# Low parts of the weights by an adding transfer instead of a subtraction on VectorE, and another order in the first stage

## The chip, the cores and the metric

The kernel runs on one core of a Trainium2 chip. The metric is the device time of one execution in microseconds; before the change the median of three runs is 983.17 us (983.04 to 983.79). A core has TensorE (PE, matmuls; PEld is its loading of stationary operands), VectorE (DVE), ScalarE (ACT), GpSimd (POOL) and SyncE (SP). Each works off its own instructions in order; they meet at semaphores. Transfers are issued by SP or by GpSimd and run on 16 DMA engines.

## The reference

One encoder layer on 512 tokens of width 1024, in float32: a layer norm, one input projection whose columns feed a gated convolution and attention with three groups of dilated windows, an output projection, a layer norm, a gated feed-forward block with a convolution, and a last layer norm.

```python
h = layer_norm(x, ln0_g, ln0_b)
proj = h @ w_in + b_in
y_a = (gate_b * dwconv3(gate_c * hin, conv_w)) @ w_a
# attention: three groups, combined with softmax weights over their denominators
y_b = comb.reshape(bsz, seq, ATT_GROUP_W) @ w_b
mix = (g_a * y_a + g_b * y_b) @ w_o + b_o
h = layer_norm(ALPHA * h + mix, ln1_g, ln1_b)
up = h @ w_up + b_up
f = gelu(dwconv3(a, ffn_conv_w) + ffn_conv_b) * gte
h = layer_norm(ALPHA * h + f @ w_down + b_down, ln2_g, ln2_b)
```

## The kernel before

Every matmul operand is a float32 value held as two fp32r values, a high part (hi) and a low part (lo, the value minus hi). A product is three matmuls, high x high, high x low, low x high (`mm3`, L357 to L360); a unit is 8 such triples over the depth of 1024, 24 matmuls of 512 columns.

The weights lie in memory as 82 chunks (0 to 81) of 2048 columns (some of 1536) in the order of use. A chunk is two halves of 1024 columns. `load` (L265) has SP fetch the halves into `raw`, three buffers. `split` (L279) has ScalarE copy a half into `hi` (L292; three buffers of 2048 columns), and `low` (L297) has VectorE write `lo = raw - hi` (L298; five buffers of 1024 columns). `chunk` (L304) is called where a chunk is first used: it splits this one and the next and loads the one after. A buffer that is taken again waits until TensorE has finished with its old content: the low half that comes five halves later. Only the last chunk's low halves lie in buffers of their own (`blk`).

Stages: first layer norm and the first four units, which take the tokens in two halves of 256 (`first_norm`, `first_features`, `first_products`; chunks 0 and 1); the rest of the input projection with attention jobs between its units (`slot`, L696); the convolution branch; the branch projections and gates; the output projection (chunks 44 to 47, blocks of 128 tokens); the feed-forward block in two parts of 11 pairs of units (chunks 48 on), each followed by its part of the down projection. In the output projection's second half and in the last stage (chunks 79 to 81) a block of 128 tokens goes through several chunks before the next block does.

A scheduler orders the instructions of each engine, except those marked with `pin`, which keep the order of the program; in the first stage most are pinned. In the first stage `feature_major` (L348) turns transposed x into features: ScalarE writes `lnT`, VectorE casts it to the high part (for half of the features of the first tokens ScalarE does, L352), and VectorE subtracts (L355). An attention job has its scores computed (`a`), is scaled (`b`), transposed (`b2`, copied by ScalarE to `PT`) and summed (`c`), in different steps of `slot`.

Of the kernel before, what the change touches and what calls it, by code (L numbers as in the profile page):

```python
# [7 lines left out]
AF = mybir.ActivationFunctionType  # L8
ALU = mybir.AluOpType
AX = mybir.AxisListType  # L10

P = 128
D = 1024
T = 512
KT = D // P
# [14 lines left out]
C_G0 = C_BIN + 76  # L30
# [57 lines left out]
def lay_out_weights(w):  # L88

    w_in, w_a, w_b, w_o = w["w_in"][0], w["w_a"][0], w["w_b"][0], w["w_o"][0]  # L90
    w_up, w_down = w["w_up"][0], w["w_down"][0]

    def block(m, f0, nf):
        k = m.shape[0] // P
        return m[:, f0 : f0 + nf].reshape(k, P, nf).transpose(1, 0, 2).reshape(P, k * nf)

    units = in_units()
    parts = []
    for name, key, cols in chunk_plan():
        if name == "in":  # L100
            c = [block(w_in, units[key + i][3] * P, P) for i in range(2)]
        elif name == "vt":
            g, kh = key
            c = [block(w_in[kh * 512 : (kh + 1) * 512], (BLK_V + g * 4) * P, 512)]
        elif name == "wa":
            c = [block(w_a, (key + i) * P, P) for i in range(2)]
        elif name == "wb":
            c = [block(w_b, (key + i) * P, P) for i in range(4)]
        elif name == "gate":
            c = [block(w_in, (BLK_GA + key) * P, P), block(w_in, (BLK_GB + key) * P, P)]  # L110
        elif name == "wo":
            half, kh = key
            c = [block(w_o[kh * 512 : (kh + 1) * 512], half * 512, 512)]
        elif name == "up":
            c = [block(w_up, key * P, P), block(w_up, DFF + key * P, P)]
        else:
            part, half, c0, n = key
            k0 = (part * FFH + c0) * P
            c = [block(w_down[k0 : k0 + n * P], half * 512, 512)]
        c = np.concatenate(c, axis=1)  # L120
        assert c.shape == (P, cols), (name, key, c.shape)
        parts.append(np.ascontiguousarray(c).reshape(-1))
    return np.concatenate(parts)
# [49 lines left out]
def build(tc, x, wst, colt, dist, rows, vrow, out):  # L173
# [3 lines left out]
    with ExitStack() as ctx:  # L177
# [22 lines left out]
        def ps(tag):  # L200
            return psum.tile([P, 512], F32, tag=tag, name="ps_" + tag, bufs=2)
# [55 lines left out]
        def col(c):  # L257
            return cols[:, c : c + 1]
# [19 lines left out]
        def split(i):  # L278
            if i >= len(plan) or i in splits:  # L279
                return  # L280
            load(i)
            n = plan[i][2]
            hi = whl.tile([P, 2048], F32R, tag="hi", name=f"hi{i}")
            if i == len(plan) - 1:
                los = [blk(F32R, (1024,), f"lo{i}") for _ in range(0, n, 1024)]
            else:
                los = [whl.tile([P, 1024], F32R, tag="lo", name=f"lo{i}", bufs=5) for _ in range(0, n, 1024)]
            step = 512 if i == 0 else 1024
            starts = (0, 1024, 512, 1536) if i == 0 else range(0, n, step)
            for c in starts:  # L290
                part = slice(c, min(c + step, n))
                nc.scalar.activation(hi[:, part], Pieces(raws[i])[:, part], AF.Copy)  # L292
                if i > 1:
                    low(i, hi, Pieces(los), part)
            splits[i] = (hi, Pieces(los))

        def low(i, hi, lo, part):  # L297
            ins = nc.vector.tensor_tensor(lo[:, part], Pieces(raws[i])[:, part], f(hi[:, part]), op=ALU.subtract)  # L298
            if i < 2:
                pin(ins)  # L300
# [3 lines left out]
        def chunk(name, key):  # L304
            i = where[(name, key)]
            split(i)
            split(i + 1)
            load(i + 2)
            return splits[i]
# [4 lines left out]
        def pin(ins):  # L314

            return tc.keep_in_program_order(ins) if pinned[0] else ins
# [28 lines left out]
        def normalise(z, mean, rstd):  # L345
            pin(nc.vector.tensor_scalar(z, z, mean, rstd, op0=ALU.subtract, op1=ALU.mult))

        def feature_major(pst, dst, kt, cg, cb, c0, c1, cast=False):  # L348
            t = f32t("lnT")[:, : c1 - c0]
            nc.scalar.activation(t, pst, AF.Identity, bias=col(cb + kt), scale=col(cg + kt))  # L350
            if cast:
                nc.scalar.activation(dst[:, 0, c0:c1], pst, AF.Identity, bias=col(cb + kt), scale=col(cg + kt))  # L352
            else:
                pin(nc.vector.tensor_copy(dst[:, 0, c0:c1], t))
            return pin(nc.vector.tensor_tensor(dst[:, 1, c0:c1], t, f(dst[:, 0, c0:c1]), op=ALU.subtract)).ins  # L355

        def mm3(o, ah, al, bh, bl, start, stop):  # L357
# [27 lines left out]
        def first_features(hf):  # L385
            rr = (2 * hf, 2 * hf + 1)
            for k0 in range(0, KT, 2):
                if hf == 0 and k0 % 4 == 0:

                    for n in range(2):  # L390
                        low(0, *splits[0], slice(n * 1024 + k0 * P, n * 1024 + (k0 + 4) * P))
                pst = ps(("pt", "s")[k0 // 2 % 2])
                for k in (k0, k0 + 1):
                    for r in rr:
                        o = pst[:, (k % 2) * 256 + (r % 2) * P :][:, :P]
                        nc.tensor.transpose(o, xt[r][:, k * P : (k + 1) * P], ident)
                for k in (k0, k0 + 1):
                    c = (k % 2) * 256
                    last = feature_major(pst[:, c : c + 256], hT[k], k, C_G0, C_B0, hf * 256, hf * 256 + 256, hf == 0 and k >= 4)
            return last  # L400

        def first_products(hf, n0, steps):
            w = splits[n0 // 2]
            t = slice(hf * 256, hf * 256 + 256)
            for n, k, m in steps:
                a = slice(n % 2 * 1024 + k * P, n % 2 * 1024 + (k + 1) * P)
                wk, hk = w[m // 2][:, a], hT[k][:, m % 2, t]
                nc.tensor.matmul(first[n][:, t], wk, hk, start=k == 0 and m == 0, stop=k == KT - 1 and m == 2)  # L408


        halves = []
# [5 lines left out]
        whole = [[(n, k, m) for k in range(KT) for m in range(3)] for n in range(4)]  # L417
        first_norm(0)
        with tc.issue_after(roots[0]):
            chunk("in", 0)  # L420
        first_features(0)
        first = [ps("acc"), ps("acc"), ps("u"), ps("u")]
        first_products(0, 0, halves)
        first_norm(1)
# [268 lines left out]

        wait, ready = [0], {}

        def slot(new=True):  # L696

            while vtodo:
                transpose_v(*vtodo.pop(0))
            if running:  # L700
                running.pop(0).c()
            if scaled:
                jb = scaled.pop(0)
                jb.b2()
                running.append(jb)
            if sums and ready[sums[0].key[0]] <= wait[0]:
                jb = sums.pop(0)
                jb.b()
                scaled.append(jb)
            if scores and new:  # L710
                for _ in range(2):
                    jb = scores.pop(0)
                    jb.a()
                p = jb.key[0]
                if not any(x.key[0] == p for x in scores) and jb.key[1] == 2:
                    merge(p)
                    ready[p] = wait[0] + 3
                    order = [(0, 0), (0, 1), (0, 2), (0, 3), (1, 0), (2, 0), (1, 1), (2, 1)]
                    sums.extend(alljobs[(p,) + o] for o in order)
            wait[0] += 1  # L720
            if new:
                scores.extend(late)
                late.clear()

        alljobs = {}
        for n, (kind, a0, a1, blkno) in enumerate(in_units()):
            w = chunk("in", n - n % 2)
            if n < 4:
                o = first[n]
            else:  # L730
                o = ps("acc")
                unit(o, w, (n % 2) * 1024, hT)
            slot()
            if kind == "v" and a0 > 0:
                slot(False)
            if kind in "qkv":
                evac_qkv(kind, a0, a1, blkno, o)
                if kind == "k":
                    for i in range(4 if a1 == 0 else 2):
                        alljobs[a0, a1, i] = Job(a0, a1, i)  # L740
                        late.append(alljobs[a0, a1, i])
                elif kind == "v":
                    vtodo.append((a0, a1))
            else:
                evac_conv(kind, a0, blkno, o)
            if n - 1 in V_AFTER:
                g = V_AFTER[n - 1]
                ws = [chunk("vt", (g, kh)) for kh in range(2)]
                for j in range(4):
                    o = values(g, j, ws)  # L750
                    slot()
                    evac_values(g, j, o)
# [203 lines left out]
```

## Time and profile before

| | |
|---|---|
| median of three runs | 983.17 us |
| profiled execution | 983.07 us |
| its span, first to last instruction | 981.3 us |
| TensorE busy | 964.7 us (98%) |
| VectorE busy | 551.1 us (56%) |
| ScalarE busy | 395.9 us (40%) |
| GpSimd busy | 55.3 us (6%) |
| bytes moved by transfers | 97.29 MB |
| mean granted TensorE clock | 0.998 |

The profile is of one execution. Busy time leaves out register, branch and semaphore instructions and those that issue transfers. Matmuls overlap each other: a 512-column matmul is listed with 0.39 us though one starts every 0.23 us. In a line of the trace, `lo<-raw,hi` is what is written and from what; an entry in square brackets is idle time of the engine before the instruction and what ended it.

### The profile page before, as it was taken

To read this page: it belongs to the slowest core of one execution; us is meant where nothing else is said; L and a number is where in the kernel's file an instruction comes from. 1 tells how busy PE (TensorE), PEld (TensorE's weight loads), DVE (VectorE), ACT (ScalarE), POOL (GpSimd) and SP (SyncE) were. 2 spreads that over 40 slices of the span, in tenths; PEclk is the share of its full clock that TensorE was granted. 3 is DMA by queue.
4 is the path that set the end of the run, shared out by engine and by line. 5 is a ranking of instruction groups with operands and counts; after the bars stand their busy time and mean duration, and the time that the engine had idled before them with its cause. 6 is when DMAs were issued, how large, how long until landed. Compare 5 with 4: busy or idle time off the path is not lost.

```text
span 981.3 us, 11983 instructions
## 1 busy us (share of the span) xinstructions
PE 964.7 (98%) x4713; PEld 813.5 (83%) x4713; DVE 551.1 (56%) x882; ACT 395.9 (40%) x675; POOL 55.3 (6%) x163
## 2 busy tenths in 40 slices
PE   8999999999999999999999999999999999999996
PEld 7888888788888888888888888988888888888885
DVE  6855855868675454421344667659452245454266
ACT  5553555565653333223433333544441134443220
POOL 1000000000010101001000000011000001000000
PEclk9999999999999999999999999999999999999999
DMA  7313322121222222326333321342323232322312
GB/s 276 103 50 129 96 77 66 65 88 65 65 65 86 87 86 86 107 86 214 108 106 109 108 84 46 129 171 84 110 75 97 86 129 93 101 86 96 129 38 81
DMA packets 28217, 97.29 MB, mean 99 GB/s; under 512 B 3456, under 2 KB 3968, under 8 KB 28160
## 3 DMA queue, kind: packets, MB, share of 16 engines
q1 hardware_dynamic: 25776, 89.60, 27.6%
q0 software_dynamic: 2384, 6.92, 2.2%
q8 instruction: 37, 0.61, 0.2%
q14 instruction: 20, 0.16, 0.1%
HBM read 94.36 MB, written 2.15 MB: 98 GB/s over the span
## 4 chain that ended last, share of the span: by engine, by line
PE 92%; DVE 3%; ACT 2%; DMA 2%; issue 1%; SPq 0%; DVEq 0%; ACTq 0%; POOLq 0%
PE ps_acc L358 15%; PE ps_acc L360 15%; PE ps_acc L359 15%; PE ps_u L358 5%; PE ps_s L360 5%; PE ps_s L358 5%; PE ps_s L359 5%; PE ps_u L360 5%; PE ps_u L359 5%; PE ps_pt L360 4%; PE ps_pt L358 4%; PE ps_pt L359 4%; PE ps_pt L580 1%; DMA raw<-wst 1%; PE ps_acc L408 1%
## 5 line engine op out<-in xcount | busy, mean ns | idle before, releaser
L298 DVE TENSOR_TENSOR lo<-raw,hi 128x1024 fp32r<-128x1024 f32 (+1 forms) x166 | 198.3, 1199 | 236.4 <-ACT hi L292 102.0
L292 ACT ACTIVATE hi<-raw 128x1024 fp32r<-128x1024 f32 (+1 forms) x166 | 166.9, 1034 | 248.4 <-PE ps_acc L359 73.5
L358 PE MATMUL ps_acc<-hT,hi 128*128 128x512 f32 x416 | 164.3, 395 | 0.6 <-DVE kbd L470 0.6
L360 PE MATMUL ps_acc<-hT,lo 128*128 128x512 f32 x416 | 162.3, 390 | 0.0
L359 PE MATMUL ps_acc<-hT,hi 128*128 128x512 f32 x416 | 162.0, 390 | 0.0
L360 PEld LDWEIGHTS ps_acc<-hT,lo 128*128 128x128 f32 x416 | 78.1, 188 | 16.7
L358 PEld LDWEIGHTS ps_acc<-hT,hi 128*128 128x128 f32 x416 | 78.2, 188 | 16.5 <-PE ps_pt L580 0.8
L359 PEld LDWEIGHTS ps_acc<-hT,hi 128*128 128x128 f32 x416 | 78.2, 188 | 15.5
L561 ACT ACTIVATE S<-S,nm 128x128 f32<-128x128 f32 (+2 forms) x96 | 40.1, 419 | 39.8 <-DVE nm L559 36.3
L359 PE MATMUL ps_acc<-h1T,hi 128*128 128x512 f32 (+1 forms) x96 | 36.0, 375 | 0.0
L358 PE MATMUL ps_acc<-h1T,hi 128*128 128x512 f32 (+1 forms) x96 | 35.8, 373 | 0.0
L358 PE MATMUL ps_pt<-h1T,hi 128*128 128x512 f32 (+1 forms) x96 | 35.6, 371 | 0.0
L359 PE MATMUL ps_pt<-h1T,hi 128*128 128x512 f32 (+1 forms) x96 | 35.6, 371 | 0.0
L360 PE MATMUL ps_pt<-h1T,lo 128*128 128x512 f32 (+1 forms) x96 | 35.6, 371 | 0.0
L358 PE MATMUL ps_u<-h1T,hi 128*128 128x512 f32 (+1 forms) x96 | 35.6, 371 | 0.0
L359 PE MATMUL ps_u<-h1T,hi 128*128 128x512 f32 (+1 forms) x96 | 35.6, 371 | 0.0
L360 PE MATMUL ps_u<-h1T,lo 128*128 128x512 f32 (+1 forms) x96 | 35.6, 371 | 0.0
L359 PE MATMUL ps_s<-h1T,hi 128*128 128x512 f32 (+1 forms) x96 | 35.6, 371 | 0.0
L358 PE MATMUL ps_s<-h1T,hi 128*128 128x512 f32 (+1 forms) x96 | 35.6, 371 | 0.0
L360 PE MATMUL ps_acc<-h1T,lo 128*128 128x512 f32 (+1 forms) x96 | 35.6, 371 | 0.0
L360 PE MATMUL ps_s<-h1T,lo 128*128 128x512 f32 (+1 forms) x96 | 35.6, 371 | 0.0
L659 POOL COPY fp<-fp 128x127 f32<-128x127 f32 x22 | 14.0, 635 | 318.0 <-ACT fp L885 318.0
(397 smaller groups left out, 2037.1 us busy)
## 6 DMA issues: line engine op xcount, KB each, us to landing
raw<-wst SPq DMA_DIRECT2D x160, 512.0 KB, 3.6
x<-x SPq DMA_DIRECT2D x4, 512.0 KB, 7.1
hb<-x POOLq DMA_DIRECT2D x4, 512.0 KB, 6.1
out<-hb SPq DMA_DIRECT2D x7, 256.0 KB, 2.1
ln_g<-rows POOLq DMA_DIRECT2D x3, 512.0 KB, 6.1
ln_b<-rows POOLq DMA_DIRECT2D x3, 512.0 KB, 6.9
raw<-wst SPq DMA_DIRECT2D x4, 256.0 KB, 2.6
vbias<-vrow POOLq DMA_DIRECT2D x1, 512.0 KB, 8.1
```

What stands on the lines that cost most here:

```text
L292: nc.scalar.activation(hi[:, part], Pieces(raws[i])[:, part], AF.Copy)
L298: ins = nc.vector.tensor_tensor(lo[:, part], Pieces(raws[i])[:, part], f(hi[:, part]), op=ALU.subtract)
L358: nc.tensor.matmul(o, ah, bh, start=start, stop=False)
L359: nc.tensor.matmul(o, ah, bl, start=False, stop=False)
L360: nc.tensor.matmul(o, al, bh, start=False, stop=stop)
L408: nc.tensor.matmul(first[n][:, t], wk, hk, start=k == 0 and m == 0, stop=k == KT - 1 and m == 2)
L561: nc.scalar.activation(v, v, AF.Exp, bias=nm[:, j : j + 1], scale=0.125, accum_out=dn[:, j : j + 1])
L580: nc.tensor.transpose(pt[:, j * P : (j + 1) * P], self.pe[:, j * P : (j + 1) * P], ident)
L659: nc.gpsimd.tensor_copy(u[:, 1:128], u[:, 512:639])
```

## The change

`split` no longer calls `low` for chunks 2 to 81. After each copy to `hi`, ScalarE writes the negated value into `lo`, rounded as `hi` is, so it is minus the high part, and GpSimd issues a transfer of the same weights from memory that adds to what stands in `lo`. Chunks 0 and 1 still go through VectorE. Chunk 0 is laid out by quarters, so that its first half holds the first four depth tiles of both units; its second half is copied to `hi` after the first four features; its low parts are made a quarter at a time; VectorE makes all casts of the features. The first products are pinned by their first matmul, chunk 1 is split after the first features, and chunk 2 is loaded there. `slot` finishes all running jobs and takes one scaling step, or two after the units of v, where there was an extra step without scores.

```diff
+            if key == 0:
+                c = [b[:, h : h + 512] for h in (0, 512) for b in c]
...
-            step = 512 if i == 0 else 1024
-            starts = (0, 1024, 512, 1536) if i == 0 else range(0, n, step)
-            for c in starts:
-                part = slice(c, min(c + step, n))
+            if i == 0:
+                splits[i] = (hi, Pieces(los))
+                return
+            for c in range(0, n, 1024):
+                part = slice(c, min(c + 1024, n))
                 nc.scalar.activation(hi[:, part], Pieces(raws[i])[:, part], AF.Copy)
                 if i > 1:
-                    low(i, hi, Pieces(los), part)
+                    l = Pieces(los)[:, part]
+                    nc.scalar.activation(l, Pieces(raws[i])[:, part], AF.Copy, scale=-1.0)
+                    src = wst[int(offs[i]) : int(offs[i + 1])].rearrange("(p c) -> p c", p=P)
+                    nc.gpsimd.dma_start(out=l, in_=src[:, part], accum_op=ALU.add)
             splits[i] = (hi, Pieces(los))
+
+        def first_high(half):
+
+            for n in range(2):
+                part = slice(half * 1024 + n * 512, half * 1024 + (n + 1) * 512)
+                pin(nc.scalar.activation(splits[0][0][:, part], Pieces(raws[0])[:, part], AF.Copy))
...
-            nc.scalar.activation(t, pst, AF.Identity, bias=col(cb + kt), scale=col(cg + kt))
-            if cast:
-                nc.scalar.activation(dst[:, 0, c0:c1], pst, AF.Identity, bias=col(cb + kt), scale=col(cg + kt))
-            else:
-                pin(nc.vector.tensor_copy(dst[:, 0, c0:c1], t))
+            pin(nc.scalar.activation(t, pst, AF.Identity, bias=col(cb + kt), scale=col(cg + kt)))
+            pin(nc.vector.tensor_copy(dst[:, 0, c0:c1], t))
...
-                if hf == 0 and k0 % 4 == 0:
-
-                    for n in range(2):
-                        low(0, *splits[0], slice(n * 1024 + k0 * P, n * 1024 + (k0 + 4) * P))
+                if hf == 0:
+
+                    if k0 == 4:
+                        first_high(1)
+                    c = k0 // 4 * 1024 + k0 // 2 % 2 * 512
+                    low(0, *splits[0], slice(c, c + 512))
...
-            chunk("in", 0)
+            split(0)
+            first_high(0)
         first_features(0)
+        split(1)
+        load(2)
...
-            if running:
+            while running:
                 running.pop(0).c()
-            if scaled:
+            while scaled:
                 jb = scaled.pop(0)
                 jb.b2()
                 running.append(jb)
-            if sums and ready[sums[0].key[0]] <= wait[0]:
-                jb = sums.pop(0)
-                jb.b()
-                scaled.append(jb)
+            for _ in range(more):
+                if sums and ready[sums[0].key[0]] <= wait[0]:
+                    jb = sums.pop(0)
+                    jb.b()
+                    scaled.append(jb)
...
-            slot()
-            if kind == "v" and a0 > 0:
-                slot(False)
+            slot(2 if kind == "v" and a0 > 0 else 1)
```

How the instructions stand on ScalarE at the start, before: `hi0` is the high part of chunk 0, `lnT` the features that come out of the transposes in `ps_pt` and `ps_s`.

```order
L330 ACTIVATE l00mv_179<-l00mv_179,eps_98 128x2
L292 ACTIVATE hi0_191<-raw0_86 128x512 x2
L292 ACTIVATE hi0_191<-raw0_89 128x512 x2
L350 ACTIVATE lnT_214<-ps_pt_209,cols_78 128x256
L350 ACTIVATE lnT_218<-ps_pt_209,cols_78 128x256
L350 ACTIVATE lnT_227<-ps_s_222,cols_78 128x256
L350 ACTIVATE lnT_231<-ps_s_222,cols_78 128x256
```

The same place on ScalarE now:

```order
L342 ACTIVATE l00mv_179<-l00mv_179,eps_98 128x2
L307 ACTIVATE hi0_191<-raw0_86 128x512 x2
L362 ACTIVATE lnT_202<-ps_pt_197,cols_78 128x256
L362 ACTIVATE lnT_206<-ps_pt_197,cols_78 128x256
L362 ACTIVATE lnT_216<-ps_s_211,cols_78 128x256
L362 ACTIVATE lnT_220<-ps_s_211,cols_78 128x256
L307 ACTIVATE hi0_191<-raw0_89 128x512 x2
```

The two copies of the second half of `raw0` have moved behind the first four features.

On ScalarE behind the first units, before: `kbd0` holds the keys, `vT00` the first values, which TensorE transposes next, `hi3` the high part of chunk 3.

```order
L468 ACTIVATE kbd0_104<-ps_acc_264,cols_78 64x4x128 x2
L292 ACTIVATE hi3_591<-raw3_442 128x1024
L474 ACTIVATE vT00_551<-ps_u_265,cols_78 128x4x112
L475 ACTIVATE vT00_551<-ps_u_265,cols_78 128x4x16
L292 ACTIVATE hi3_591<-raw3_444 128x1024
```

And now:

```order
L485 ACTIVATE kbd0_104<-ps_acc_264,cols_78 64x4x128 x2
L295 ACTIVATE hi3_593<-raw3_444 128x1024
L298 ACTIVATE lo3_594<-raw3_444 128x1024
L491 ACTIVATE vT00_553<-ps_u_265,cols_78 128x4x112
L492 ACTIVATE vT00_553<-ps_u_265,cols_78 128x4x16
L295 ACTIVATE hi3_593<-raw3_446 128x1024
```

The negated part of chunk 3 (L298) stands between the keys and the values.

On ScalarE at the end, before: the high parts of the last chunks, 79 to 81.

```order
L292 ACTIVATE hi79_7340<-raw79_7288 128x1024
L292 ACTIVATE hi79_7340<-raw79_7290 128x1024
L292 ACTIVATE hi80_7395<-raw80_7347 128x1024
L292 ACTIVATE hi80_7395<-raw80_7349 128x1024
L292 ACTIVATE hi81_7406<-raw81_7402 128x1024
L292 ACTIVATE hi81_7406<-raw81_7404 128x512
```

And now, with the negated parts:

```order
L298 ACTIVATE lo79_7496<-raw79_7444 128x1024
L298 ACTIVATE lo80_7552<-raw80_7503 128x1024
L295 ACTIVATE hi80_7551<-raw80_7503 128x1024
L295 ACTIVATE hi80_7551<-raw80_7505 128x1024
L298 ACTIVATE lo81_7565<-raw81_7560 128x1024
L298 ACTIVATE lo81_7566<-raw81_7562 128x512
L298 ACTIVATE lo80_7553<-raw80_7505 128x1024
L295 ACTIVATE hi81_7564<-raw81_7560 128x1024
```

The second low half of chunk 80 stands behind both of chunk 81, and GpSimd's transfers to them stand in the same order.

## Rows read from the trace of the kernel before

**Rows 1.** Page, part 1: span, and each engine's busy us (share) xinstructions
```profile
span 981.3 us, 11983 instructions
...
PE 964.7 (98%) x4713; PEld 813.5 (83%) x4713; DVE 551.1 (56%) x882; ACT 395.9 (40%) x675; POOL 55.3 (6%) x163
```

**Rows 2.** Waits of PE: who waited for whom: us in total, times, longest us
```profile
PE ps_pt L396 <- DVE x L346: 2.2, 2, 1.1
PE ps_u L358 <- ACT PT L582: 2.1, 2, 1.6
PE ps_u L408 <- ACT hi L292: 1.1, 1, 1.1
```

**Rows 3.** Windows: the stretch, then each engine's busy us in it
```profile
core 0: us, PE busy (x) PEld busy (x) DVE busy (x) ACT busy (x) POOL busy (x), PEclk, DMA share, GB/s
10.00:30.00 20.00, 16.75 (x128) 15.17 (x128) 15.07 (x34) 11.71 (x21) 0.40 (x2) 1.00 0.52 205
...
120.00:250.00 130.00, 127.13 (x664) 107.86 (x663) 91.42 (x184) 76.09 (x181) 6.14 (x14) 1.00 0.23 72
...
635.00:930.00 295.00, 295.00 (x1304) 244.36 (x1303) 143.69 (x159) 110.19 (x140) 23.17 (x83) 1.00 0.33 107
```

**Rows 4.** Lines: groups, busy us, mean ns; third row from 120 to 250 us
```profile
L298 DVE TENSOR_TENSOR lo<-raw,hi 128x1024 fp32r<-128x1024 f32 (+1 forms) x166 | 198.3, 1199 | 236.4 <-ACT hi L292 102.0 <-PE ps_acc L360 50.6 <-PE ps_s L359 28.6
L292 ACT ACTIVATE hi<-raw 128x1024 fp32r<-128x1024 f32 (+1 forms) x166 | 166.9, 1034 | 248.4 <-PE ps_acc L359 73.5 <-PE ps_s L360 48.3 <-PE ps_u L360 39.7
L292 ACT ACTIVATE hi<-raw 128x1024 fp32r<-128x1024 f32 x18 | 18.6, 1058 | 13.7 <-PE ps_acc L359 9.8 <-issue 2.9 <-ACT S L561 0.9
```

**Rows 5.** Timeline of PE, ACT and DVE, first stage: start, duration, what
```profile
10.77 0.55 PE L396 MATMUL ps_pt<-cols,x 128*128 128x128 f32 x3
...
11.23 1.15 ACT L292 ACTIVATE hi<-raw 128x512 fp32r<-128x512 f32 x2 [2.04 <-DMA raw<-wst]
12.29 1.00 ACT L350 ACTIVATE lnT<-ps_pt,cols 128x256 f32<-128x256 f32 x2
...
10.63 0.68 DVE L298 TENSOR_TENSOR lo<-raw,hi 128x512 fp32r<-128x512 f32 x1
...
12.87 0.29 DVE L354 CAST hT<-lnT 128x256 fp32r<-128x256 f32 x1 [0.28 <-ACT lnT L350]
...
13.54 0.28 DVE L354 CAST hT<-lnT 128x256 fp32r<-128x256 f32 x1
...
20.64 1.28 DVE L319 BATCH_NORM_STATS2 l02st<-x 128x6 f32<-128x512 f32 x2
...
40.53 1.08 ACT L474 ACTIVATE vT<-ps_u,cols 128x448 f32<-128x448 f32 x1
...
41.81 0.64 PE L484 MATMUL ps_pt<-cols,vT 128*128 128x128 f32 x4
```

**Rows 6.** Transfers: queue total; issue of two hb loads; landings; the first load from GpSimd
```profile
q1 hardware_dynamic: 25776, 89.60, 27.6%
...
L810 POOL DMA_DIRECT2D hb<-x x2: 528/530/531, 485.2 to 519.4; - x2
...
DMA to landing us min/median/max: 4.1/4.4/4.7
...
vbias<-vrow POOLq DMA_DIRECT2D x1, 512.0 KB, 8.1
```

**Rows 7.** Timeline of PE in the output projection: last and first uses of low halves
```profile
584.44 0.39 PE L359 MATMUL ps_u<-lo,mix 128*128 128x512 f32 x1
...
590.56 0.39 PE L359 MATMUL ps_acc<-lo,mix 128*128 128x512 f32 x1
...
605.26 0.39 PE L359 MATMUL ps_u<-lo,mix 128*128 128x512 f32 x1
...
612.93 0.28 PE L360 MATMUL ps_s<-h1T,lo 128*128 128x256 f32 x1
```

**Rows 8.** Timeline of PE in the last stage: last and first use
```profile
941.35 0.39 PE L359 MATMUL ps_u<-lo,f 128*128 128x512 f32 x1
...
946.79 0.39 PE L359 MATMUL ps_acc<-lo,f 128*128 128x512 f32 x1
```

More of the change, by code (lines that the diff above doesn't have):

```diff
@@ L346, in normalise, with feature_major @@
             pin(nc.vector.tensor_scalar(z, z, mean, rstd, op0=ALU.subtract, op1=ALU.mult))
-        def feature_major(pst, dst, kt, cg, cb, c0, c1, cast=False):
+        def feature_major(pst, dst, kt, cg, cb, c0, c1):
             t = f32t("lnT")[:, : c1 - c0]
-            nc.scalar.activation(t, pst, AF.Identity, bias=col(cb + kt), scale=col(cg + kt))
-            if cast:
-                nc.scalar.activation(dst[:, 0, c0:c1], pst, AF.Identity, bias=col(cb + kt), scale=col(cg + kt))
-            else:
-                pin(nc.vector.tensor_copy(dst[:, 0, c0:c1], t))
+            pin(nc.scalar.activation(t, pst, AF.Identity, bias=col(cb + kt), scale=col(cg + kt)))
+            pin(nc.vector.tensor_copy(dst[:, 0, c0:c1], t))
             return pin(nc.vector.tensor_tensor(dst[:, 1, c0:c1], t, f(dst[:, 0, c0:c1]), op=ALU.subtract)).ins
@@ L398, in first_features @@
                     c = (k % 2) * 256
-                    last = feature_major(pst[:, c : c + 256], hT[k], k, C_G0, C_B0, hf * 256, hf * 256 + 256, hf == 0 and k >= 4)
+                    last = feature_major(pst[:, c : c + 256], hT[k], k, C_G0, C_B0, hf * 256, hf * 256 + 256)
             return last
@@ L405, in first_products @@
             for n, k, m in steps:
-                a = slice(n % 2 * 1024 + k * P, n % 2 * 1024 + (k + 1) * P)
+                c = n % 2 * 1024 + k * P if n >= 2 else k // 4 * 1024 + n * 512 + k % 4 * P
+                a = slice(c, c + P)
                 wk, hk = w[m // 2][:, a], hT[k][:, m % 2, t]
-                nc.tensor.matmul(first[n][:, t], wk, hk, start=k == 0 and m == 0, stop=k == KT - 1 and m == 2)
+                ins = nc.tensor.matmul(first[n][:, t], wk, hk, start=k == 0 and m == 0, stop=k == KT - 1 and m == 2)
+                if hf == 0 and k == 0 and m == 0:
+                    pin(ins)
         halves = []
@@ L694, in build, with slot @@
         wait, ready = [0], {}
-        def slot(new=True):
+        def slot(more=1):
             while vtodo:
                 transpose_v(*vtodo.pop(0))
-            if running:
+            while running:
                 running.pop(0).c()
-            if scaled:
+            while scaled:
                 jb = scaled.pop(0)
@@ L705, in slot @@
                 running.append(jb)
-            if sums and ready[sums[0].key[0]] <= wait[0]:
-                jb = sums.pop(0)
-                jb.b()
-                scaled.append(jb)
-            if scores and new:
+            for _ in range(more):
[3 more added lines that the diff above has]
+                    scaled.append(jb)
+            if scores:
                 for _ in range(2):
@@ L720, in slot @@
             wait[0] += 1
-            if new:
-                scores.extend(late)
-                late.clear()
+            scores.extend(late)
+            late.clear()
         alljobs = {}
```

## The prediction

> **What bounds the kernel now.** I read the busy times first, then who TensorE waited for, then the stages, then the places where a low part of a weight is made and used. TensorE is busy 964.7 of 981.3 us [rows 1]; the next engine, VectorE, 551.1. So TensorE's stream of matmuls sets the time, and a change can give back only its gaps and what stands around the stream. The waits say where gaps are: 2.2 us for the normalised x and 1.1 us for a high part, both in the first 30 us, and 2.1 us for the transposed attention weights [rows 2]. By stages [rows 3]: 3.25 us idle from 10 to 30 us, 2.87 us from 120 to 250 us, none from 635 to 930 us, all at a granted clock of 1.00 (2.4 GHz). The span of the profiled execution is 981.3 us and its time 983.07, so 1.8 us lie outside; the median of the runs shown, 983.17, is 0.1 us above it. I add to 983.07. About 0.2% (2 us) is what a measurement of this kernel can tell from no change.
>
> **What goes, and what it is worth.** Of 166 subtractions on VectorE, 160 go: 160 x 1.2 us, about 191 us of busy time [rows 4]. VectorE isn't what TensorE waits for, except at the start and around the attention weights, so these 191 us are hidden now, under the matmuls, and taking them away is worth nothing by itself. In their place ScalarE writes 160 negated high parts. They have the form of the copies that write the high parts, 1.03 us each [rows 4], so 165 us, and ScalarE goes from 396 to about 561 us of 981: still hidden on average. GpSimd issues 160 transfers (156 of 512 KB, 4 of 256 KB), at 0.53 us each [rows 6] some 85 us.
>
> **Start.** The high parts of the second half of chunk 0 no longer stand in front of the first transposed features on ScalarE. Those wait for the transposes, done at 10.77 + 0.55 = 11.32; in the trace ScalarE writes hi until 12.38 and begins at 12.29 [rows 5]. So the first cast on VectorE moves from 12.87 to about 11.9. From there VectorE now has eight pairs of cast and subtraction (0.67 us a pair, 12.87 to 13.54) and three of the 0.68 us low parts: 5.4 + 2.0 = 7.4 us, so the statistics of the second half of x start at about 19.3 instead of 20.64 [rows 5], and all that hangs on them (the 2.2 us wait among it) comes 1.3 us earlier. But at 40.53 ScalarE writes vT, for which TensorE's transposes start at 41.81 with no time to spare [rows 5], and one negated part of 1.03 us now stands in front of it. Net 0.3 us gained; 1.3 if the negated part moved out of the way, nothing if another wait comes up.
>
> **Attention, 120 to 250 us.** 18 halves of chunks are split here [rows 4]. VectorE gives up 18 x 1.2 = 21.6 us of 91.4, ScalarE takes 18 x 1.03 = 18.5 us on top of 76.1 in 130 us [rows 3]. ScalarE works in order, and a negated part that waits for its buffer holds up the copies of attention weights behind it, which TensorE does wait for [rows 2]. The ends are 2.9 us gained (all of today's idle time) and 18.5 us lost (each negated part in front of a copy that is waited for). I take zero: between the transposes of a job and the matmuls that use its copies lies a unit of matmuls, as before, and a unit is 24 x 0.226 = 5.4 us, more than a few instructions of 1 us.
>
> **The new wait: how long the low part takes.** A low part was ready 1.2 us after its buffer came free. Now it is a negated part (1.03 us), an issue on GpSimd, and a transfer that reads the destination as well. The trace shows no adding transfer. Plain ones of 512 KB from GpSimd, alone, landed 4.1 and 4.7 us after their issue, 0.53 us of issuing included, and 8.1 us under the first loads [rows 6]. One pass of 512 KB over the 16 engines takes 8 packets each, 27.6% x 16 x 981.3 us / 25776 = 0.168 us a packet, so 1.35 us [rows 6]. The ends are 4.1 us (the second read costs nothing) and 8.1 + 1.35 = 9.5 us. I take 4.4 + 1.35 = 5.75 us, one more pass on the mean of the two lone ones, the nearest rows.
> The Trainium skill, Collectives: The Full Stack, section on the bandwidth ceiling, says that an adding transfer halves the rate because it needs two source reads, not because the add costs cycles; no row here shows it, and by it the extra pass is the 1.35 us that I took.
> The Trainium skill, DMA: Bandwidth & Descriptors, section on the anatomy of a DMA from GpSimd, gives 2.0 us plus bytes / 436e3 for one, an estimate of 3.2 us for 512 KB; the trace differs with 4.1 and 4.7, and decides. With the page's figure and one more pass the two stalls below come to 0.5 us.
>
> Where is there room for 5.75 us? In the feed-forward stage five low buffers stand in a row, and a half is used for 24 matmuls of 0.226 us (295 us / 1304) [rows 3]: from the release of a buffer to the use of its next content four halves pass, 21.7 us, less 1.03. That covers even 9.5 us. Room is short where halves are used side by side:
> - Output projection. A buffer's last use starts at 584.44 and its next content is first used at 590.56 [rows 7]: 590.56 - (584.44 + 0.39 + 1.03) = 4.7 us, so 1.05 us late. The next: 612.93 - (605.26 + 0.39 + 1.03) = 6.25 us, just in time.
> - Last stage. 946.79 - (941.35 + 0.39 + 1.03) = 4.0 us [rows 8], so 1.75 us late, and all of it goes to the end: the rest of this row block and the three others come behind it.
> In the last stage ScalarE now does the part of chunk 80 that has to wait after both parts of chunk 81, which are free early, so those lie out of the way.
>
> **The rest.** The raw weights are read twice, so some 83 MB more. In the feed-forward stage the engines are busy 0.33 of a chunk of 48 x 0.226 = 10.9 us, 3.6 us [rows 3]; two adding transfers of two passes make it 9.0. It fits. GpSimd's shifts for the convolutions stand between these issues and wait for ScalarE; a transfer held up behind one has its 20 us of room, so nothing. If that cover goes, the wait lands on TensorE whole. Two attention jobs a step instead of one plus an extra step: the same instructions, nothing.
>
> **Sum:** 983.07 - 0.3 + 0 + 1.05 + 1.75 = 985.6 us.
>
> **Rivals.**
> 1. *Faster.* The transfer takes no longer than the shortest plain one (4.1 us: late by 0 and 0.1), the start keeps its 1.3 us, and VectorE's relief closes the attention's 2.9 us: 983.07 + 0.1 - 1.3 - 2.9 = 979.0. For it: VectorE writes the low half of the transposed attention weights, and low parts of the weights stand in its queue there. Against: the transfer has more to do than a plain one.
> 2. *Slower by more: the transfer lands late under load.* At 9.5 us the output projection loses 4.8, then 3.25 (its release moves along with the stall), the last stage 5.5: 983.07 - 0.3 + 13.55 = 996.3. For it: 8.1 us at the start, where the queues were full. Against: 4.1 and 4.7 where they were not, and the two short places lie in stages with few loads. It is slower from 4.0 us on, and by over 2 us from some 5.5.
> 3. *The DMA engines run out.* With three passes to an adding transfer a chunk needs 3.6 + 2 x 3 x 1.35 = 11.7 us of engine time against 10.9: 80 x 0.8 = 64 us, 1047 us; from 2.7 passes on it decides everything. For it: it is not far off. Against: a read and a write of a plain transfer overlap already.
> 4. *Nothing.* The stalls and the gains cancel, as they do with a transfer of 4.5 to 5 us: 0.5 to 1.0 us lost at the end, 0 to 0.3 in the projection, less the 0.3 at the start: 0.2 to 1.0 us, 983.7.
>
> **How the numbers follow.** Forecast 0.38, and 0.08 of this lies within 2 us of before, since the sum is 2.5 us. Rival 1 0.29, of which 0.23 faster by more than 2 us and 0.06 within. Rival 2 0.14, rival 3 0.06, rival 4 0.13. So faster 0.23, same 0.08 + 0.06 + 0.13 = 0.27, slower 0.30 + 0.14 + 0.06 = 0.50. The forecast's own range is 983.5 to 989. The range for eight in ten goes from 979.5 (near rival 1) to 997 (rival 2) and leaves out rival 3 and the lower edge of rival 1.
>
> **What would show it.** In the profile after: adding transfers of about 5.8 us to landing (4.4 would speak for rival 1, 9 for rival 2) and a DMA share of about 0.8 in the feed-forward stage; TensorE waiting for a low part's transfer near 590 and 947 us and nowhere in the feed-forward stage; its first product about 1 us earlier; its transposes of vT waiting for ScalarE; ScalarE near 560 us busy, VectorE near 360. Waits for transfers in the feed-forward stage, or a longer wait for attention weights on ScalarE, would prove the forecast wrong.

## The result, and the profile after

The changed kernel takes 1017.94 us (median of four, 1015.25 to 1020.37) against 983.2: ratio 1.0352, 95% interval 1.0328 to 1.0377. It is slower by 3.5%, far outside the forecast's range. The profiled execution took 1020.37 us, its span is 1018.5.

The page's first part after, answering to [rows 1]:

```profile
span 1018.5 us, 12213 instructions
...
PE 980.2 (96%) x4713; PEld 821.8 (81%) x4713; DVE 367.5 (36%) x726; ACT 541.8 (53%) x831; POOL 182.1 (18%) x323
```

VectorE and ScalarE moved about as forecast (360 and 560). What counts is TensorE: the span grew by 37.2 us. Its idle time went from 981.3 - 964.7 = 16.6 to 1018.5 - 980.2 = 38.3 us, so 21.7 us more. The other 15.5 us are *busy* time, for the same 4713 matmuls; the mean granted clock is 0.984, where it was 0.998.

Who TensorE waited for, answering to [rows 2] (us in total, times, longest):

```profile
PE ps_acc L368 <- DMA lo<-wst: 15.7, 6, 7.0
PE ps_acc L367 <- DVE kbd L487: 3.3, 2, 1.6
PE ps_s L369 <- DMA lo<-wst: 2.0, 1, 2.0
PE ps_u L368 <- DVE PT L600: 2.0, 2, 1.6
PE ps_pt L369 <- DMA lo<-wst: 1.8, 1, 1.8
PE ps_pt L597 <- DVE v L505: 1.6, 1, 1.6
...
PE ps_pt L501 <- ACT vT L492: 0.7, 1, 0.7
```

Nearly 20 us are waits for the adding transfers. The stages, answering to [rows 3] (PE busy first, then its granted clock, the share of the DMA engines and GB/s at the end):

```profile
10.00:30.00 20.00, 19.23 (x140) 16.94 (x140) 17.38 (x44) 12.50 (x22) 1.07 (x2) 1.00 0.75 259
120.00:250.00 130.00, 127.26 (x641) 107.33 (x639) 65.11 (x150) 92.56 (x190) 23.68 (x35) 0.97 0.72 158
635.00:930.00 295.00, 292.23 (x1366) 245.47 (x1367) 83.38 (x119) 161.60 (x200) 65.86 (x141) 0.99 0.87 200
```

And the transfers, answering to [rows 6] (the add queue, then median us from issue to landing of the raw loads and of the adding ones):

```profile
q0 software_dynamic: 25424, 89.76, 47.2%
...
raw<-wst SPq DMA_DIRECT2D x160, 512.0 KB, 5.7
lo<-wst POOLq DMA_DIRECT2D x156, 512.0 KB, 7.9
```

An adding transfer lands after 7.9 us in the median, where 5.75 were taken, and the raw loads take 5.7, where they took 3.6 before.

Where the 37 us arise is seen by comparing the start of the same matmul, by its number from the first, before and after. The lag at these points, worked out from the two timelines of TensorE:

| stretch (us, after) | lag gained | forecast |
|---|---|---|
| start, to 46 | -0.6 | -0.3 |
| input projection, 46 to 124 | +9.2 | 0 |
| input projection, 124 to 148 | +6.2 | 0 |
| 148 to 600 | -0.1 | 0 |
| output projection, 605 to 615 | +6.3 | +1.05 |
| first units behind it, 633 to 648 | +5.7 | 0 |
| 648 to 970 | 0.0 | 0 |
| last stage, 972 to 987 | +10.6 | +1.75 |

These are the lags of one execution, the slowest of the four. Other executions share them out a little differently: in experiment 4, whose code differs only from chunk 80 on, the input projection loses 12.2 us and not 15.4.

**The start went as forecast.** Columns: start, duration, what. The first cast on VectorE was to move from 12.87 to about 11.9, and the product to wait at vT behind the negated part; all three rows are of the kernel after (VectorE, ScalarE, TensorE), answering to [rows 5]:

```profile
11.97 0.29 DVE L363 CAST hT<-lnT 128x256 fp32r<-128x256 f32 x1 [0.64 <-ACT lnT L362]
...
38.89 1.04 ACT L298 ACTIVATE lo<-raw 128x1024 fp32r<-128x1024 f32 x1
...
41.20 0.66 PE L501 MATMUL ps_pt<-cols,vT 128*128 128x128 f32 x4 [0.74 <-ACT vT L492]
```

The lead is 1.5 us before vT and 0.6 behind it.

**Output projection.** The place where 1.05 us was forecast, TensorE, answering to [rows 7]; between two rows lie three matmuls, but for the wait in the third row.

```profile
603.90 0.39 PE L368 MATMUL ps_acc<-lo,mix 128*128 128x512 f32 x1
604.58 0.39 PE L368 MATMUL ps_acc<-lo,mix 128*128 128x512 f32 x1
608.93 0.80 PE L368 MATMUL ps_acc<-lo,mix 128*128 128x512 f32 x1 [3.52 <-DMA lo<-wst]
610.38 0.63 PE L368 MATMUL ps_acc<-lo,mix 128*128 128x512 f32 x1
611.66 0.63 PE L368 MATMUL ps_s<-lo,mix 128*128 128x512 f32 x1
```

The transfer was issued at 600.92 and landed 8.0 us later. With 8.0 in place of 5.75 the prediction's own sum gives 8.0 - 4.7 = 3.3 us of wait; TensorE waits 3.5 us. But the lag grows by 6.3. The rest is the clock; windows behind the stall, columns as above:

```profile
609.00:614.00 5.00, 5.00 (x12) 3.95 (x13) 2.18 (x7) 0.30 (x1) 0.00 (x0) 0.50 0.48 129
615.00:620.00 5.00, 5.00 (x24) 4.12 (x23) 1.87 (x4) 0.00 (x0) 0.00 (x0) 1.00 0.00 0
```

TensorE stood idle for 3.5 us, and the granted clock is 0.50 (1.2 GHz) in the five us behind it, where three matmuls take 1.28 us (610.38 to 611.66) instead of 0.68 (603.90 to 604.58); later it is 1.00 (2.4 GHz) again. This is the busy time that grew.

**Input projection.** No stall was forecast here. ScalarE near 90 us:

```profile
88.65 1.06 ACT L295 ACTIVATE hi<-raw 128x1024 fp32r<-128x1024 f32 x1 [5.75 <-DMA raw<-wst]
89.62 1.38 ACT L485 ACTIVATE kbd<-ps_acc,cols 64x512 fp32r<-64x512 f32 x2
```

ScalarE stands 5.75 us waiting for a *raw load*, and the copy of the keys (`kbd`) stands behind it. TensorE waits for the keys (1.64 us), then at 97 and 101 us for low parts. The transfers issued from 76 to 84 us, raw loads and adding ones (four of each, median us to landing):

```profile
raw<-wst SPq DMA_DIRECT2D x4, 512.0 KB, 11.0
lo<-wst POOLq DMA_DIRECT2D x4, 512.0 KB, 12.1
```

Four halves are wanted in quick succession here, and eight transfers share the same 16 engines. At 131 us it repeats (ScalarE waits 6.0 us for a raw load, keys and PT behind it).

**Last stage.** TensorE, answering to [rows 8], then ScalarE:

```profile
974.47 0.40 PE L367 MATMUL ps_acc<-hi,f 128*128 128x512 f32 x1
981.86 0.79 PE L368 MATMUL ps_acc<-lo,f 128*128 128x512 f32 x1 [7.00 <-DMA lo<-wst]
```

```profile
964.79 1.06 ACT L298 ACTIVATE lo<-raw 128x1024 fp32r<-128x1024 f32 x1 [0.86 <-DMA raw<-wst]
972.60 1.58 ACT L298 ACTIVATE lo<-raw 128x512 fp32r<-128x512 f32 x2 [6.75 <-DMA raw<-wst]
```

The two at 972.60 are the second part of chunk 81 and, behind it, the part of chunk 80 that TensorE needs next. The one in front waited 6.75 us for its raw load; the transfer of the needed one was issued at 974.47, and TensorE wanted it at 974.70. Here too the clock falls with the wait (a window, columns as above):

```profile
980.00:985.00 5.00, 3.14 (x7) 2.48 (x8) 0.00 (x0) 0.00 (x0) 0.00 (x0) 0.50 0.06 12
```

### The profile page after: what moved, and what is told of

It reads as the page before. It is cut to its first block, busy times and chain, and to the rows that moved or that the text cites. A ratio compares the mean times of both kernels' runs of the same rounds, so it can differ in the third digit from the quotient of the medians.

```text
span 1018.5 us, 12213 instructions
## 1 busy us (share of the span) xinstructions
PE 980.2 (96%) x4713; PEld 821.8 (81%) x4713; DVE 367.5 (36%) x726; ACT 541.8 (53%) x831; POOL 182.1 (18%) x323
## 4 chain that ended last, share of the span: by engine, by line
PE 80%; issue 7%; DMA 6%; DVE 2%; ACT 2%; POOL 1%; DVEq 0%; POOLq 0%; ACTq 0%
PE ps_acc L368 13%; PE ps_acc L367 13%; PE ps_acc L369 13%; PE ps_s L367 4%; PE ps_s L368 4%; PE ps_s L369 4%; DMA lo<-wst 4%; PE ps_u L368 4%; PE ps_u L367 4%; PE ps_u L369 4%; PE ps_pt L369 4%; PE ps_pt L367 4%; PE ps_pt L368 4%; PE ps_pt L597 1%; PE ps_u L420 1%
## 5 line engine op out<-in xcount | busy, mean ns | idle before, releaser
L300 POOL DMA_DIRECT2D lo<-wst x160 | 136.5, 855 | 624.9 <-ACT lo L298 557.1
L295 ACT ACTIVATE hi<-raw 128x1024 fp32r<-128x1024 f32 x162 | 167.8, 1043 | 130.7 <-issue 58.2
L298 ACT ACTIVATE lo<-raw 128x1024 fp32r<-128x1024 f32 (+1 forms) x160 | 166.6, 1042 | 97.3 <-PE ps_s L368 37.4
L682 DVE SCALAR_TENSOR_TENSOR cv<-fp,cols,cv 128x512 f32<-128x512 f32 x22 | 16.6, 753 | 86.7 <-ACT cv L681 86.7
L600 DVE TENSOR_TENSOR PT<-ps_pt,PT 128x512 fp32r<-128x512 f32 x32 | 22.1, 691 | 51.9 <-ACT PT L599 51.6
```

Source lines behind the costliest of these rows:

```text
L298: nc.scalar.activation(l, Pieces(raws[i])[:, part], AF.Copy, scale=-1.0)
L300: nc.gpsimd.dma_start(out=l, in_=src[:, part], accum_op=ALU.add)
L600: nc.vector.tensor_tensor(t[:, 1], pt, f(t[:, 0]), op=ALU.subtract)
L682: nc.vector.scalar_tensor_tensor(a, u[:, 128:640], col(c + step), a, op0=ALU.mult, op1=ALU.add)
```

## The experiments

Theory A: the loss is the transfers', in engine time and queueing, at places where halves follow each other quickly. Its rivals: the new attention steps (B), the fixed time of a transfer from GpSimd (C), the sheer load on the engines everywhere (G).

**1. All but the transfers.**

```diff
-                    l = Pieces(los)[:, part]
...
-                    nc.gpsimd.dma_start(out=l, in_=src[:, part], accum_op=ALU.add)
+                    low(i, hi, Pieces(los), part)
```

> The whole change except the transfers: every low part is again VectorE's subtraction; chunk 0's layout, the first stage's order and the attention steps stay as changed. Theory A (all of the loss is the transfers): the start keeps its 1.5 us, the 0.9 us at vT goes with the negated part, so about 981.5 us. Rival B (the new order of the attention steps costs the 5 to 6 us that appear between 130 and 150 us): 984 us or more, with TensorE waiting for transposed attention weights there as in the changed kernel.

979.27 us (979.11 to 979.71), ratio 0.9955 (0.9942 to 0.9967): 4.3 us less than before, clear of noise, though under half a per cent. TensorE's waits:

```profile
PE ps_pt L594 <- DVE v L502: 1.5, 1, 1.5
PE ps_pt L404 <- DMA cols<-colt: 1.2, 1, 1.2
PE ps_u L257 <- DVE warm L250: 1.1, 1, 1.1
PE ps_acc L417 <- DVE hT L360: 0.6, 2, 0.3
```

The whole loss comes with the transfers and their negated parts: 1017.94 - 979.27 = 38.7 us. B falls. It is 2 us below A's number, so the new steps gain as well (9).

**2. The transfers alone**, on the kernel before (its subtraction replaced by the negated part and the adding transfer).

> The kernel before, with nothing but the low parts of chunks 2 to 81 written as negated part plus adding transfer. Theory A: the whole loss and none of the start's gain, so 1018 to 1021 us, with the same waits near 100, 135, 605, 635 and 972 us. Rival B (the attention steps' new order makes the loss of 5 to 6 us near 135 us): 1012 to 1014 us, no stall near 135.

1020.74 us (ratio 1.0379, 1.0363 to 1.0395), with stalls near 93, 135, 606, 631 and 970 us: as A expects, and not as B does. (The stall near 135 us is smaller here: the lag grows by 3.0 us from 124 to 148 us, in the changed kernel by 6.2.)

**3. The same transfers without the add.**

```diff
-                    nc.gpsimd.dma_start(out=l, in_=src[:, part], accum_op=ALU.add)
+                    nc.gpsimd.dma_start(out=l, in_=src[:, part])
```

> The changed kernel with a plain transfer of the same bytes in place of the adding one (lo then holds the weights themselves instead of their low part; negated parts, issues and waits are the same). Theory A (the time on the 16 DMA engines decides: an adding packet takes 328 ns, a plain one 168 ns, and these queue with the raw loads): landing falls from a median of 7.9 us to 4.5 to 5.5 us, the raw loads from 5.7 to about 4, and most of the stalls go: 983 to 991 us. Rival C (fixed time decides: the negated part, 0.85 us of issue, the start of a transfer from GpSimd, ScalarE's order): landing stays over 6.5 us and the time over 1003 us.

987.05 us (ratio 1.0041, 1.0025 to 1.0056). The queue's share, and medians to landing:

```profile
q0 software_dynamic: 25424, 89.76, 28.0%
...
raw<-wst SPq DMA_DIRECT2D x160, 512.0 KB, 4.2
lo<-wst POOLq DMA_DIRECT2D x156, 512.0 KB, 5.2
```

The bytes and the number of issues are the same (each issue 0.53 us on GpSimd instead of 0.85), and 30.9 of 38.7 us are gone: the add decides, and C falls. From the shares it costs 0.472 x 1018.5 - 0.280 x 984.7 = 205 us of all 16 engines, over 158 transfers of 512 KB 1.30 us each; 1.35 was the estimate. TensorE still waits for the plain transfers at the three late places, 4.4 us in all.

**4. ScalarE's order at the end.**

```diff
+                keep = tc.keep_in_program_order if i >= 80 else (lambda ins: ins)
-                    nc.scalar.activation(l, Pieces(raws[i])[:, part], AF.Copy, scale=-1.0)
+                    keep(nc.scalar.activation(l, Pieces(raws[i])[:, part], AF.Copy, scale=-1.0))
```

(and the copy to `hi` likewise).

> The changed kernel with ScalarE kept to the order of the program for chunks 80 and 81: the negated part of the second half of chunk 80 stands ahead of chunk 81, not behind it. In the changed kernel it stood behind a part of chunk 81 that waited until 972.6 us for its raw load, and its transfer was issued at 974.5 and landed at 981.8, 7.2 us after it was wanted. Theory D (ScalarE's order is what makes the last stall): the part is written near 969, its transfer lands by 977, the last stage loses 2 to 4 us instead of 10.6, so 1010 to 1012 us. Rival A2 (the transfers themselves are too long there, whatever the order): at least 1015 us.

1008.48 us (ratio 1.0254, 1.024 to 1.0268). In the last stage TensorE now waits three times:

```profile
968.27 0.50 PE L369 MATMUL ps_acc<-lo,f 128*128 128x512 f32 x1 [0.48 <-DMA lo<-wst]
...
970.88 0.51 PE L369 MATMUL ps_acc<-lo,f 128*128 128x512 f32 x1 [0.96 <-DMA lo<-wst]
...
973.40 0.50 PE L369 MATMUL ps_acc<-lo,f 128*128 128x512 f32 x1 [0.85 <-DMA lo<-wst]
```

The lag grows by 3.2 us there instead of 10.6. With three short waits instead of one of 7 us the clock stays at 1.00 there. So some two thirds of the last stall were ScalarE's order, not the transfer's length. The time is 1.5 us below the range expected: ahead of the last stage, where the code is the changed kernel's, this execution lags 4.5 us less than the changed kernel's profiled one.

**5. Transfers only where there is room.**

```diff
+                    if i < 22 or 46 <= i <= 50 or i >= 79:
+                        low(i, hi, Pieces(los), part)
+                        continue
```

> The changed kernel, but VectorE subtracts where TensorE was seen to stall: chunks 2 to 21 (input projection), 46 to 50 (output projection and the two first units after it), 79 to 81 (end). Transfers remain for chunks 22 to 45 and 51 to 78, 104 of 160. Theory A (the loss sits only where halves are used in quick succession and a transfer queues behind others; a half with 20 us of room hides even 10 us): no wait for a transfer, 979.0 to 981.0 us, as with VectorE's low parts everywhere (979.27). Rival G (the sheer load of the DMA engines costs something everywhere, so the loss goes with the number of transfers): 104/160 of 38.7 us, over 1000 us.

979.11 us (ratio 0.9959, 0.9946 to 0.9971). Of the 104 transfers 101 are of 512 KB:

```profile
lo<-wst POOLq DMA_DIRECT2D x101, 512.0 KB, 7.8
```

They land as late as in the changed kernel, and TensorE waits for none of them. G falls: the load on the engines and a landing after 7.8 us cost nothing where a half has 20 us.

**6. Six low buffers.**

```diff
-        tmp = pool("tmp", 13)
+        tmp = pool("tmp", 11)
...
-                los = [whl.tile([P, 1024], F32R, tag="lo", name=f"lo{i}", bufs=5) for _ in range(0, n, 1024)]
+                los = [whl.tile([P, 1024], F32R, tag="lo", name=f"lo{i}", bufs=6) for _ in range(0, n, 1024)]
```

> The changed kernel with six low buffers instead of five (the pool of 512-column temporaries goes from 13 to 11 to make room). A half then has one more half's use, 5.4 us, between the release of its buffer and its next use. Theory A1 (the room after the release decides): the stalls near 605 and 635 us shrink by up to 5.4 us each to nearly nothing, the last one stays (ScalarE's order); 1000 to 1006 us. Rival H (the DMA engines are full in bursts, raw loads included, so an earlier release only queues the transfer earlier): at least 1012 us.

999.06 us (ratio 1.0159, 1.0143 to 1.0174). By the lags, the place at 605 us now costs nothing, the one behind it 4.0, the last 2.8 (ScalarE wrote the part of chunk 80 early here, so against the expectation that stall shrank too). Room decides at these places, and H falls. The input projection loses 6.8 us, where it lost 15.4 and, in experiment 4, 12.2; TensorE waits there for the keys (4.6 us in two waits) and no longer for a low part. A loss is new: against experiment 1 the lag grows by 7.7 us near 295 us, where TensorE waits 3.7 us for `cv`, a value of the convolution branch, and runs at 0.50 behind it; whether that comes of the two temporaries taken away was not tried.

**7 and 8. What one adding transfer costs.** Six adding transfers in the feed-forward stage, VectorE's low parts elsewhere; first from memory, then from the raw buffer on the chip, which the next load can take only when the transfer has landed.

```diff
+                    if not (54 <= i < 78 and i % 4 == 2 and c == 0):
+                        low(i, hi, Pieces(los), part)
+                        continue
...
-                    nc.gpsimd.dma_start(out=l, in_=src[:, part], accum_op=ALU.add)
+                    nc.gpsimd.dma_start(out=l, in_=Pieces(raws[i])[:, part], accum_op=ALU.add)
```

> VectorE's low parts everywhere but in 6 halves of the feed-forward stage (the first half of chunks 54, 58, 62, 66, 70 and 74), which take the adding transfer: its price where no other adding transfer is near, beside at most the raw loads. Theory A (a lone adding transfer costs what was estimated, 5.75 us, and the 7.9 us of the changed kernel are queueing): 5.3 to 6.0 us to landing without a raw load beside it, up to 7.2 with one; the time 979.3 us. Rival C (an adding transfer takes 7.9 us by itself): 7.5 us or more for all of them.

> As the run with 6 adding transfers, but each reads the raw buffer on the chip instead of the weights in memory. The raw buffer is then free only when the transfer has landed, so the next raw load cannot run beside it, as it did beside all 6 there (6.8 to 8.1 us to landing). Theory R (the raw load that starts with it is what lengthens it): 5.0 to 5.7 us, as the few of the changed kernel that ran alone, packets still 328 ns. Rival C (a transfer here takes 7 us or more whatever runs beside it): 6.8 us or more. Rival M (reading memory is the slow part): packets under 300 ns.

979.67 and 979.11 us, a single execution each. Landing of the six, from memory and then from the raw buffer:

```profile
DMA to landing us min/median/max: 6.8/7.5/8.1
```

```profile
DMA to landing us min/median/max: 4.5/4.5/5.0
```

The first expectation failed on both sides: there was no other adding transfer, so A wanted at most 7.2 us, and C at least 7.5 for all of them. All six had a raw load beside them (the one issued at 661.2 us had one issued at 660.5). From the raw buffer it is 4.5 to 5.0 us, at or just under R's range and far from C's, with packets of 327 to 361 ns, no shorter than from memory. Not all of these 3 us are the neighbour's, since the source changed too: two transfers of the changed kernel that read memory with next to nothing beside them (issued at 61.8 and 313.2 us) took 5.7 and 5.4 us. So some 2 us go to the neighbour and some 1 us to the source. C falls, and M with it. The neighbour is no accident: the negated part is the last reader of a raw buffer, so its end releases SP's next load and GpSimd's transfer together.

**9. The attention steps as before**, else as 1 (`while` back to `if`, the extra step back).

> VectorE's low parts everywhere and the first stage as changed, but the attention steps as before (one job finished, transposed and scaled a step, an extra step after units of v). Against e1 (979.27 us) this undoes the steps alone. Theory S (the new steps close most of the attention's idle time): 981.3 us, 1.8 us lost up to 0.84 + 0.84 + 2.0 us of gaps back between 120 and 250 us. Rival T (they do nothing, the gain is the start's and passes on): 979.0 to 979.6 us.

981.48 us (ratio 0.9981, 0.9972 to 0.999). Against experiment 1 the new steps are worth 2.2 us, as S expects. Its waits show the old gap again:

```profile
PE ps_u L364 <- ACT PT L596: 2.1, 2, 1.6
```

**10. All transfers from the raw buffer**, the second edit of 8 alone.

> The changed kernel with all 160 adding transfers reading the raw buffer on the chip instead of memory, so half the memory reads go, a transfer has no raw load of the next half beside it, and a raw buffer is held until its transfer has landed. Theory A (time on the DMA engines and room decide): landing 5 to 6.5 us, but raw loads start 5 to 6 us later, so the bursts near 100 and 135 us and the end still stall; 995 to 1025 us. Rival M (the second read of memory is what costs): packets under 300 ns, below 992 us.

1005.57 us (ratio 1.0239, 1.021 to 1.0269). Landing falls to 5.5 us, and 12 of 38.7 us come back. But raw loads start later, and ScalarE waits for them instead:

```profile
L295 ACT ACTIVATE hi<-raw 128x1024 fp32r<-128x1024 f32 x162 | 168.5, 1045 | 226.1 <-DMA raw<-wst 135.0
```

M falls: the packets are no shorter (339 ns in the median, 328 from memory), and the time is far from 992.

## Why the prediction was wrong

The prediction had these right: VectorE's relief is worth nothing (experiments 1 and 5 agree within 0.2 us with 160 and 56 subtractions); the steady part of the feed-forward stage hides the transfers at a DMA share of 0.87; the start, its gain and the wait at vT; the price of the extra pass, 1.30 us against 1.35. The Trainium skill, Collectives: The Full Stack, section on the bandwidth ceiling, says of ReduceScatter that it runs at half the rate because its add needs two source reads, not because the add costs cycles. Packets of 328 ns, against 174 for the plain ones of experiment 3 (medians), agree with the half; whether the read or the add makes it, no run here tells apart.

Four of its steps were wrong.

1. *"I take 4.4 + 1.35 = 5.75 us, one more pass on the mean of the two lone ones".* For a lone transfer that holds: 5.4 and 5.7 us for the two of the changed kernel that had next to nothing beside them. But it is hardly ever alone: 6.8 to 8.1 us beside the raw load that the same negated part releases, 12 where four are wanted in a row. The upper end (9.5 us, rival 2) was nearer, and [rows 6] held a sign of it: 8.1 us under the first loads. The step's error was that "the two short places lie in stages with few loads"; the change itself puts a load beside nearly every transfer.
2. *"Room is short where halves are used side by side"* and then only two places. The input projection was costed as ScalarE's copies alone, and only from 120 us on; with landings of 8 to 14 us its halves were short too, and raw loads, late beside the same transfers, held ScalarE and the copies behind it. This is 15.4 us, the largest part. Likewise the units behind the output projection, "just in time" at 6.25 us, lost 5.7 us: their transfers took 7.7 and 9.8 us.
3. *"both parts of chunk 81, which are free early, so those lie out of the way".* Their buffers are free early, but the raw load of the second took 9.6 us to land and held ScalarE. The last stage lost 10.6 us instead of 1.75, some 7 of it by this order (experiment 4).
4. The clock had no term. Behind the waits of 3.5 and 7 us TensorE ran at 0.50 for some us, and so it did behind shorter ones close together (1.25 and 2.19 us near 100 us, 1.98 and 1.76 us near 640 us); single waits of 1.6 us, at 252 and 311 us, had no such stretch behind them. Of the 37.2 us of span 15.5 are added busy time. With plain transfers (experiment 3), where the longest wait is 2.7 us, TensorE's busy time is 967.6 us, and no such stretch comes ahead of the end.

The attention's zero, taken for the steps and the parts together, hid two terms of opposite sign: -2.2 us for the new steps (experiment 9), and what the transfers cost there, which is a part of step 2 up to 150 us and 2.0 us more from 160 to 380 us by the lag against experiment 1.

Rival 2 had the mechanism of step 1 and the sign (996.3 us). It fell short by steps 2, 3 and 4. Not settled is how the input projection's 15.4 us divide between low parts and late raw loads: experiments 3 and 5 remove both together. Experiment 6, where the waits for low parts are gone there and 6.8 us stay, hints at a half each, but its temporaries differ too.

The best version is that of experiment 1 or 5 (979.27 and 979.11; they can't be told apart): the first stage and attention steps as changed, without transfers where room is short.

## What to carry to other kernels

Before a computation is turned into a transfer, list for each use how long it may take, and price the transfer *with what its own trigger releases at the same time*: bytes on the engines, not the time of a lone one. An instruction that waits for a transfer on an engine that works in order holds all that stands behind it, so place it behind what is needed sooner. A gap in TensorE's stream can cost nearly twice its length (3.5 us cost 6.3 here): count the slow clock behind it.

## What the runs showed of the hardware that was not expected

An adding transfer's issue on GpSimd takes 0.85 us where a plain one takes 0.53, so the 160 issues took 136.5 us and not the 85 of the prediction; GpSimd had room for them:

```profile
L300 POOL DMA_DIRECT2D lo<-wst x160: 830/847/1718, 22.1 to 974.5; - x160
```

An adding transfer's packets are no shorter when they read the chip's own buffer (experiments 8 and 10). And the loads by SP are slowed too: 3.6 us in the median in experiment 1, 4.2 with plain transfers from GpSimd (3), 5.7 with adding ones.
